# W2 of an encoder's MLP: three of its four groups in seven products with the tokens down the partitions, sums kept in DRAM, and a part of the weight splitting on GpSimd

## The chip, the cores and the metric

The kernel runs on one core of a Trainium2 chip. The metric is the device time of one execution in microseconds. Every time below is read from the runs of the kernel before or from one profiled execution of it.

## The reference

Two layers of an encoder trunk on x of 512 tokens by 1024, all in float32. A layer has an attention half (one input projection, three token mixers, gates and an output projection) and an MLP half. The change lies in the MLP half, in its second matrix, W2 (4096 x 1024):

```python
m = jnp.einsum('bsd,df->bsf', rms_norm(h, mlp_norm[l]), w_mlp_in[l])   # 1024 -> 4096
m = jnp.square(jax.nn.relu(m))
h = h + jnp.einsum('bsf,fd->bsd', m, w_mlp_out[l])                     # 4096 -> 1024
```

## The kernel before

**Numbers.** TensorE multiplies a short form of float32. So each operand is cut in two parts, hi (a cast on ScalarE, ACT) and lo (the operand minus hi, a subtraction on VectorE, DVE), and each product is three matmuls: hi by hi, hi by lo, lo by hi (`passes`, line 568). Weights come by DMA in quarters of 128 x 1024 into two `stage` buffers and are cut into `w_hi` and `w_lo` (`cut_to`, line 512; six buffers of each).

**The MLP half** (`mlp`, line 1335). First come eight units of the output projection (`wo`). Then W1 and W2 run in four groups of 1024 of the 4096 inner columns. W1 goes by pairs of units, four pairs to a group; a pair takes seven products of half size instead of eight (`pair`, line 644; Winograd's form of Strassen's). For that DVE makes sums of the weight blocks (`sa`, `sb` in `cut_pair`, line 535) and adds up the products, which leave PSUM as `c0`, `c1` (shown as `c`); a product has 12 matmuls of 256 columns, a pair 84. The first of those additions, `c<-x,pu`, reads the PSUM tile `x26`, and the pair's last product is written into the same tile.

W2 goes by units: 128 output columns by 512 tokens, eight units to a group, with the weights stationary and the tokens moving. A unit is 24 matmuls of 512 columns (`prod_a`, line 720: 8 blocks of 128 rows, three passes). ACT applies relu and square to each `c` and casts `mh`; DVE makes `ml`. Group 0 copies each unit out of PSUM to a tile `mo` (ACT); groups 1 and 2 add into it (DVE); at the end of group 2 `mo` is scaled and added to h (two more DVE additions a unit); group 3 does the same straight from PSUM and hands h on to the next layer (`ready`) or to the output.

**The order.** The program is first noted down, instruction by instruction. `Plan.order` then lets each engine take the first of its instructions that is ready by a table of costs (`price`), and the outcome is a fixed order for every engine, which the chip runs in order. `mlp_order` (line 52) weaves the first two pairs of the next group's W1 between units of W2 (`WOVEN`). The table does not hold what two engines cost each other when they run side by side.

Of the kernel before, what the change touches and what calls it, by code (L numbers as in the profile page):

```python
# [28 lines left out]
# positions of the small per-layer vectors in the row that every partition receives  # L29
# [20 lines left out]


def mlp_order():
    """W1 goes by pairs of units, W2 by units, in four groups of eight; a group's W1 starts within the W2 before it."""
    pairs = lambda g, k: [("w1", g, 2 * i) for i in k if g < 4]
    seq = pairs(0, range(4))
    for g in range(4):
        n = 0
        for i in range(8):
            while n < len(WOVEN) and WOVEN[n] == i:
                seq += pairs(g + 1, [n])  # L60
                n += 1
            seq.append(("w2", g, i))
# [4 lines left out]
def weight_plan():  # L67
    """Quarters of [128, 1024] in the order in which the core uses them: (key, matrix, rows, columns)."""
# [40 lines left out]
    for what, g, i in mlp_order():  # L109
# [18 lines left out]
AHEAD_LOAD = 6  # L128
AHEAD_SPLIT = 2
# [28 lines left out]
class Ref:  # L158
    """A view of such a tile."""
# [52 lines left out]
def price(engine, op, k):  # L212
    """About how long the engine is held, in ns."""
# [1333 lines left out]
```

## Time and profile before

| | |
|---|---|
| median of 3 runs | 1792.6 us (1791.58 to 1792.85) |
| profiled execution, span of its instructions | 1791.8 us |
| PE (TensorE) busy | 1767.7 us, 99% |
| DVE (VectorE) busy | 1376.4 us, 77% |
| ACT (ScalarE) busy | 983.2 us, 55% |
| POOL (GpSimd) busy | 297.1 us, 17% |

The profile was taken from one execution whose span is 0.8 us below the median of the timed runs. Matmuls are pipelined, so a matmul's own duration overlaps the next one; what a matmul costs is the distance from its start to the next one's. The same holds to a smaller degree for DVE and ACT. In the first layer the MLP half runs from about 518 us (first matmul of `wo`) to 898 us, in the second from 1407 us to the end. The stage just ahead of it, from 404 to 517 us, is the merge of the gates, in which GpSimd adds up gates of 512 columns (`gth`) while DVE cuts the weights of the gates' pairs.

### The profile page before, as it was taken

Reading aid. Unit: us, or ns where it says so; the run is one execution under the profiler, and the core shown is the slowest. Engines: PE = TensorE matmul, PEld = TensorE weight load, DVE = VectorE, ACT = ScalarE, POOL = GpSimd, SP = SyncE. Lnnn points to the kernel's source line nnn. Section 1 sums busy time; section 2 is a strip of 40 time slices with the busy share of each in tenths; the row PEclk is TensorE's granted clock in tenths of the full one; section 3 lists DMA queues with packets and bytes.
Section 4 is the critical chain, followed back from the end, with each engine's and each line's share of the span. In section 5 each row is a group of like instructions: output and inputs, shape, how many; then the busy total and the mean of one; then the engine's idle time right before and its main releaser. Section 6 shows DMA issues by size and latency. Waiting matters only on the chain.

```text
span 1791.8 us, 26264 instructions
## 1 busy us (share of the span) xinstructions
PE 1767.7 (99%) x10216; PEld 1544.8 (86%) x10216; DVE 1376.4 (77%) x2084; ACT 983.2 (55%) x1568; POOL 297.1 (17%) x294
## 2 busy tenths in 40 slices
PE   8999999999999999999999999999999999999999
PEld 6887888889989989999888778888888899989897
DVE  7866797899979766678656677968999797566783
ACT  5545666784446655445444455768844466444450
POOL 3334472002210000000013335700111100000000
PEclk9999999999999999999999999999999999999999
DMA  6311212112352323333432121121133423234331
GB/s 203 105 61 49 93 49 79 59 37 95 107 170 101 118 94 118 123 115 116 152 106 71 48 80 62 59 63 56 39 104 130 159 83 134 95 102 128 121 113 56
DMA packets 53691, 172.50 MB, mean 96 GB/s; under 512 B 6336, under 2 KB 6848, under 8 KB 53568
## 3 DMA queue, kind: packets, MB, share of 16 engines
q1 hardware_dynamic: 53568, 170.84, 29.4%
q8 instruction: 80, 1.31, 0.3%
q14 instruction: 43, 0.35, 0.1%
HBM read 162.43 MB, written 8.39 MB: 95 GB/s over the span
## 4 chain that ended last, share of the span: by engine, by line
PE 82%; DVE 8%; issue 3%; POOL 3%; ACT 2%; DMA 1%; SPq 0%; DVEq 0%; ACTq 0%; POOLq 0%
PE x L411 21%; PE w L411 20%; PE gate L411 6%; PE proj L411 5%; PE wo L411 5%; PE c L411 4%; PE wtr L413 2%; PE rv L411 2%; DVE w_lo L417 2%; PE rg L411 2%; PE rq L411 2%; PE dsc L411 2%; PE gav L411 2%; PE gsc L411 2%; DVE c L417 1%
## 5 line engine op out<-in xcount | busy, mean ns | idle before, releaser
L417 ACT CAST w_hi<-stage 128x1024 fp32r<-128x1024 f32 (+1 forms) x283 | 276.6, 982 | 319.7 <-PE w L411 120.7
L417 DVE TENSOR_TENSOR w_lo<-stage,w_hi 128x1024 fp32r<-128x1024 f32 (+1 forms) x283 | 336.9, 1192 | 78.7 <-ACT w_hi L417 75.8
L411 PE MATMUL x<-u,w_hi 128*128 128x256 f32 x1472 | 273.5, 284 | 5.3 <-DVE c L417 5.3
L411 PEld LDWEIGHTS x<-u,w_hi 128*128 128x128 f32 x1472 | 232.3, 192 | 10.9 <-DVE c L417 8.2
L411 PE MATMUL x<-u,w_lo 128*128 128x256 f32 x736 | 208.0, 283 | 0.0
L411 PE MATMUL w<-ml,w_hi 128*128 128x512 f32 (+1 forms) x520 | 200.3, 386 | 0.0
L411 PE MATMUL w<-mh,w_lo 128*128 128x512 f32 (+1 forms) x520 | 200.1, 386 | 0.0
L411 PE MATMUL w<-mh,w_hi 128*128 128x512 f32 (+1 forms) x520 | 200.1, 387 | 0.0
L411 PEld LDWEIGHTS x<-u,w_lo 128*128 128x128 f32 x736 | 141.1, 192 | 0.0
L417 ACT ACTIVATE c<-c 128x512 f32<-128x512 f32 x156 | 98.4, 631 | 32.9 <-DVE c L417 30.2
L411 PEld LDWEIGHTS w<-mh,w_lo 128*128 128x128 f32 x520 | 97.8, 188 | 19.5
L411 PEld LDWEIGHTS w<-ml,w_hi 128*128 128x128 f32 x520 | 97.8, 188 | 18.7
L411 PEld LDWEIGHTS w<-mh,w_hi 128*128 128x128 f32 x520 | 97.8, 188 | 18.5
L411 PE MATMUL gate<-u,w_hi 128*128 128x512 f32 x320 | 107.3, 399 | 0.0
L411 PE MATMUL x<-t23h,w_lo 128*128 128x256 f32 x368 | 104.2, 283 | 0.0
L411 PE MATMUL x<-t23l,w_hi 128*128 128x256 f32 x368 | 104.0, 283 | 0.0
L411 PE MATMUL x<-t23h,w_hi 128*128 128x256 f32 x368 | 103.9, 283 | 0.0
L417 ACT CAST w_hi<-sa 128x1024 fp32r<-128x1024 f32 x46 | 48.5, 1053 | 77.0 <-DVE sa L417 55.9
L411 PE MATMUL c<-w_hi,u 128*128 128x512 f32 x256 | 86.1, 394 | 0.0
L417 POOL TENSOR_TENSOR gth<-gth,c 128x512 f32<-128x512 f32 x28 | 45.9, 1647 | 179.0 <-DVE c L417 179.0
L417 DVE TENSOR_TENSOR c<-x,pu 128x512 f32<-128x512 f32 x92 | 63.1, 686 | 12.0 <-PE x L411 11.3
L411 PEld LDWEIGHTS x<-t23l,w_hi 128*128 128x128 f32 x368 | 70.6, 192 | 0.0
(278 smaller groups left out, 4554.5 us busy)
## 6 DMA issues: line engine op xcount, KB each, us to landing
stage<-in_w SPq DMA_DIRECT2D x283, 512.0 KB, 3.6
h<-in_x SPq DMA_DIRECT2D x16, 256.0 KB, 5.3
mid<-h SPq DMA_DIRECT2D x16, 256.0 KB, 2.0
h<-mid SPq DMA_DIRECT2D x16, 256.0 KB, 4.8
keep<-h SPq DMA_DIRECT2D x8, 256.0 KB, 4.1
h<-keep SPq DMA_DIRECT2D x8, 256.0 KB, 3.9
out<-h SPq DMA_DIRECT2D x7, 256.0 KB, 2.0
t_ret<-in_t_ret SPq DMA_DIRECT2D x4, 256.0 KB, 4.9
```

The lines of the kernel that those rows point to most:

```text
L411: self.nc.tensor.matmul(k.pop("out"), **k)
L413: self.nc.tensor.transpose(k["out"], k["in_"], k["identity"])
L417: getattr(getattr(self.nc, o.engine), o.name)(**k)
```

## The change

In groups 0, 1 and 2 the eight units of W2 become one product of 1024 by 1024 in seven products of half size (`wide_product`). Now the tokens are stationary, 128 at a time down the partitions, and the weights move, 512 columns at a time. Each of the seven gives 256 tokens by 512 columns, in two PSUM tiles of 128 tokens, with 12 matmuls of 512 columns for each tile, 24 in all. Group 3 stays as it was.

- **Weights** (`cut_wide`): the four blocks A11, A12, A21, A22 of a group's W2 are loaded once, in pieces of 512 columns, and the sums S1 to S4 are made in place on DVE. The hi parts are cast on ACT. The lo parts of the plain blocks A11, A12, A22 (`BESIDE`) are subtracted on GpSimd, 12 pieces to a group; those of the sums on DVE.
- **Tokens** (`rights`): the sums of the token blocks are made in place on DVE, in pieces of 256 columns, and then split into `xh` and `xl`. `mh` and `ml` are gone in these groups.
- **Results**: ACT copies each PSUM tile to `wp`. In group 0 it is stored to DRAM (`sums`) by a DMA of SyncE's queue; in groups 1 and 2 a DMA that GpSimd issues adds it to what lies there. In group 3 `gather` loads the 14 sums back, combines them on DVE (14 additions), turns them with 32 transposes of 128 x 128 on TensorE, and adds to h.
- **Order**: the woven pairs of W1 stand after the second and fourth of the seven products, and the loads are noted where a weight is cut.

```diff
-WOVEN = (3, 6)
+GATHERED = (0, 3)
+WIDE_GROUPS = (0, 1, 2)
+WOVEN = {True: (2, 4), False: (3, 6)}
...
+        elif g not in WIDE_GROUPS:
             a_unit(("w2", g, i), "w_mlp_out", cols(i * 128, 128), r0=g * 1024)
+        elif i == 0:
+            for c in range(2):
+                for j in range(2):
+                    for k in range(2):
+                        r = g * 1024 + j * 512 + k * 256
+                        plan.append((("w2", g, c + 1, j + 1, k), "w_mlp_out", np.arange(r, r + 256), cols(c * 512, 512)))
...
+WIDE = ("A11", "A12", "A22", "S1", "S2", "S4", "S3")
+WIDE_PRODUCTS = (1, 2, 4, 5, 6, 3, 7)
+BESIDE = ("A11", "A12", "A22")
...
+    def cut_wide(self, q, op, k):
+        raw = self.raw
+        def load(x):
+            at = q + (int(x[1]) - 1) * 4 + (int(x[2]) - 1) * 2 + k
+            raw[x, k] = [self.g(x) for _ in range(2)]
+            for i, t in enumerate(raw[x, k]):
+                self.nc.sync.dma_start(out=t, in_=self.a["w"][at][:, i * 512:(i + 1) * 512])
+        def add(x, y):
+            for t, o in zip(raw[x, k], raw[y, k]):
+                self.nc.vector.tensor_tensor(out=t, in0=t, in1=o, op=ALU.add)
+        for x in {"A11": ("A11", "A12"), "A12": ("A22",), "A22": ("A21",)}.get(op, ()):
+            load(x)
+        x = {"S1": "A22", "S2": "A22", "S4": "A12", "S3": "A21"}.get(op, op)
+        if op[0] == "S":
+            add(x, {"S1": "A21", "S2": "A11", "S4": "A22", "S3": "A11"}[op])
+        hi, lo = self.parts(self.p_w, 1024)
+        for i, t in enumerate(raw[x, k]):
+            c = slice(i * 512, i * 512 + 512)
+            self.nc.scalar.copy(out=hi[:, c], in_=t)
+            (self.nc.gpsimd if op in BESIDE else self.nc.vector).tensor_tensor(out=lo[:, c], in0=t, in1=hi[:, c], op=ALU.subtract)
+        return hi, lo
...
-        total = [None] * 8
-        ms = [([], []) for _ in range(4)]
+        ms = [[] for _ in range(4)]
         for what, g, i in mlp_order():
             m = ms[g]
             if what == "w1":
...
                 for c in cs:
                     nc.scalar.activation(out=c, in_=c, func=AF.Relu)
                     nc.scalar.activation(out=c, in_=c, func=AF.Square)
-                    hi, lo = self.g("mh", F32R), self.g("ml", F32R)
-                    self.split(c, hi, lo)
-                    m[0].append(hi)
-                    m[1].append(lo)
+                    if g in WIDE_GROUPS:
+                        m.append(c)
+                        continue
+                    m.append((self.g("mh", F32R), self.g("ml", F32R)))
+                    self.split(c, *m[-1])
                 continue
-            if g == 2:
-                for k in range(3) if i == 0 else range(i + 2, min(i + 3, 8)):
-                    h[k] = load(mid, k)
+            if g in WIDE_GROUPS:
+                if i == 0:
+                    rights = self.rights(m)
+                    nxt = next(rights)
+                now, nxt = nxt, next(rights, None)
+                self.wide_product(l, g, i, now)
+                continue
+            if i == 0:
+                gather = self.gather(h, mid, load, r2)
+            if i in GATHERED:
+                next(gather)
             hi, lo = self.weights(l, ("w2", g, i))
-            if g == 3 and i == 7 and l == L - 1:
-                self.last_unit(hi, lo, m, r2, h[i], ready)
+            m2 = [x[0] for x in m], [x[1] for x in m]
+            if i == 7 and l == L - 1:
+                self.last_unit(hi, lo, m2, r2, h[i], ready)
                 continue
             p = self.psum("mm", "w2")
-            for _ in self.prod_a(p, hi, lo, m, 8, 128):
+            for _ in self.prod_a(p, hi, lo, m2, 8, 128):
                 pass
-            if g == 0:
-                total[i] = self.g("mo")
-                nc.scalar.copy(out=total[i], in_=p)
-            elif g < 3:
-                nc.vector.tensor_tensor(out=total[i], in0=total[i], in1=p, op=ALU.add)
-                if g == 2:
-                    nc.vector.tensor_tensor(out=total[i], in0=total[i], in1=r2, op=ALU.mult)
-                    nc.vector.tensor_tensor(out=h[i], in0=h[i], in1=total[i], op=ALU.add)
+            y = self.g("y")
+            nc.vector.tensor_tensor(out=y, in0=p, in1=r2, op=ALU.mult)
+            nc.vector.tensor_tensor(out=h[i], in0=h[i], in1=y, op=ALU.add)
+            ready(i, h[i])
...
+    def rights(self, m):
+        nc = self.nc
+        lt, rt = slice(0, 256), slice(256, 512)
+        sub = lambda out, x, y: nc.vector.tensor_tensor(out=out, in0=x, in1=y, op=ALU.subtract)
+        t1 = []
+        for n in WIDE_PRODUCTS:
+            if n == 4:
+                for j in range(4):
+                    b1, b2 = m[j], m[4 + j]
+                    if j % 2 == 0:
+                        t1.append(self.g("t1"))
+                    sub(b1[:, rt], b2[:, rt], b1[:, rt])
+                    nc.vector.tensor_tensor(out=b1[:, lt], in0=b1[:, rt], in1=b1[:, lt], op=ALU.add)
+                    sub(b2[:, lt], b2[:, lt], b1[:, lt])
+                    sub(t1[-1][:, j % 2 * 256:j % 2 * 256 + 256], b2[:, rt], b1[:, lt])
+            out = []
+            for i in range(2):
+                hi, lo = self.g("xh", F32R), self.g("xl", F32R)
+                if n == 5:
+                    self.split(t1[i], hi, lo)
+                else:
+                    for j in range(2):
+                        k = 2 * i + j
+                        x = m[k if n in (1, 6, 7) else 4 + k][:, lt if n in (1, 2, 4, 6) else rt]
+                        c = slice(j * 256, j * 256 + 256)
+                        self.split(x, hi[:, c], lo[:, c])
+                out.append((hi, lo))
+            yield out
...
+    def wide_product(self, l, g, o, x):
+        nc, n = self.nc, WIDE_PRODUCTS[o]
+        ps = [self.psum("mm", f"wide{n}") for _ in range(2)]
+        for k in range(2):
+            hi, lo = self.weights(l, ("w2", g, o), k)
+            xh, xl = x[k]
+            for s in range(2):
+                for j in range(2):
+                    t = slice(j * 256 + s * 128, j * 256 + s * 128 + 128)
+                    c = slice(j * 512, j * 512 + 512)
+                    self.passes(ps[s], [(xh[:, t], hi[:, c]), (xh[:, t], lo[:, c]), (xl[:, t], hi[:, c])],
+                                k == 0 and j == 0, k == 1 and j == 1)
+        for s, p in enumerate(ps):
+            y = self.g("wp")
+            nc.scalar.copy(out=y, in_=p)
+            if g == WIDE_GROUPS[0]:
+                nc.sync.dma_start(out=self.sums[n, s], in_=y)
+            else:
+                nc.gpsimd.dma_start(out=self.sums[n, s], in_=y, accum_op=ALU.add)
...
+    def gather(self, h, mid, load, r2):
+        nc = self.nc
+        def back(n, s):
+            x = self.g("wp")
+            nc.sync.dma_start(out=x, in_=self.sums[n, s])
+            return x
+        tt = lambda out, x, y, op=ALU.add: nc.vector.tensor_tensor(out=out, in0=x, in1=y, op=op)
+        u2, c = [None, None], [[None] * 4, [None] * 4]
+        for s in range(2):
+            p1, p2, p6, p5, p3 = (back(n, s) for n in (1, 2, 6, 5, 3))
+            tt(p2, p1, p2)
+            tt(p6, p6, p1, ALU.subtract)
+            tt(p5, p5, p6)
+            tt(p3, p3, p5, ALU.subtract)
+            c[0][s], c[0][2 + s], u2[s] = p2, p3, (p6, p5)
+        for half in range(2):
+            if half:
+                for s in range(2):
+                    p7, p4 = back(7, s), back(4, s)
+                    p6, p5 = u2[s]
+                    tt(p5, p5, p7, ALU.subtract)
+                    tt(p6, p6, p7, ALU.subtract)
+                    tt(p6, p6, p4)
+                    c[1][s], c[1][2 + s] = p6, p5
+            for i in range(4):
+                k = half * 4 + i
+                h[k] = load(mid, k)
+                p = self.psum("tr", "turn")
+                for t in range(4):
+                    self.transpose(p[:, t * 128:(t + 1) * 128], c[half][t][:, i * 128:(i + 1) * 128])
+                y = self.g("y")
+                nc.vector.tensor_tensor(out=y, in0=p, in1=r2, op=ALU.mult)
+                nc.vector.tensor_tensor(out=h[k], in0=h[k], in1=y, op=ALU.add)
+            yield
```

Below, three places in the two kernels' orders. On TensorE, where the first group of W2 in the first layer begins (`x` is a product of W1, `w` one of W2, `wide` one of the seven), before:

```order
L411 MATMUL x_6388<-u_6000,w_lo 128x256
L411 MATMUL w_6498<-mh,w_hi 128x512
L411 MATMUL w_6498<-ml,w_hi 128x512
L411 MATMUL w_6498<-mh,w_lo 128x512
L411 MATMUL w_6498<-mh,w_hi 128x512
L411 MATMUL w_6498<-ml,w_hi 128x512
```

and after:

```order
L457 MATMUL x_6454<-u_6024,w_lo 128x256
L457 MATMUL wide_6562<-w_hi,xh 128x512
L457 MATMUL wide_6562<-w_lo,xh 128x512
L457 MATMUL wide_6562<-w_hi,xl 128x512
L457 MATMUL wide_6562<-w_hi,xh 128x512
L457 MATMUL wide_6562<-w_lo,xh 128x512
```

The unit `w` has become one of the two tiles of the product `wide`; the shape of a matmul, 128 x 512, has stayed.

On GpSimd, from the last gate of the first layer on, before:

```order
L417 TENSOR_TENSOR gth<-gth,c_5507 128x512
L417 TENSOR_TENSOR gth<-gth,c_5568 128x512
L417 TENSOR_SCALAR vmu<-vsum 128x4
L417 TENSOR_TENSOR rs<-ms,mhalf 128x4
L417 TENSOR_SCALAR vmu<-vsum 128x4 x3
```

and after, in the second group, from the fourth piece of A12 on (`A` is a piece of a weight block):

```order
L463 TENSOR_TENSOR w_lo<-A_7110,w_hi 128x512
L463 DMA sums_101<-wp 128x512
L463 DMA sums_102<-wp 128x512
L463 TENSOR_TENSOR w_lo<-A_7216,w_hi 128x512
L463 TENSOR_TENSOR w_lo<-A_7242,w_hi 128x512
L463 TENSOR_TENSOR w_lo<-A_7231,w_hi 128x512
L463 DMA sums_103<-wp 128x512
L463 DMA sums_104<-wp 128x512
L463 TENSOR_TENSOR w_lo<-A_7249,w_hi 128x512
```

Where GpSimd had nothing to do between the gates and the next layer's first unit, it has 36 subtractions and 28 adding DMAs to a layer.

On DVE, ahead of one of the additions `c<-x,pu` in the second group, before:

```order
L417 TENSOR_TENSOR mo<-mo,w_7305 128x512
L417 TENSOR_TENSOR w_lo<-stage,w_hi 128x1024
L417 TENSOR_TENSOR mo<-mo,w_7366 128x512
L417 TENSOR_TENSOR w_lo<-stage,w_hi 128x1024
L417 TENSOR_TENSOR mo<-mo,w_7407 128x512
L417 TENSOR_TENSOR w_lo<-stage,w_hi 128x1024 x2
L417 TENSOR_TENSOR c_7499<-x_7455,pu 128x512
```

and after:

```order
L463 TENSOR_TENSOR A_7242<-A_7242,A_7591 128x512
L463 TENSOR_TENSOR w_lo<-stage,w_hi 128x512
L463 TENSOR_TENSOR A_7231<-A_7231,A_7571 128x512
L463 TENSOR_TENSOR xl<-t_7449,xh 128x512
L463 TENSOR_TENSOR w_lo<-A_7216,w_hi 128x512
L463 TENSOR_TENSOR xl<-t_7593,xh 128x512
L463 TENSOR_TENSOR w_lo<-A_7242,w_hi 128x512
L463 TENSOR_TENSOR c_7736<-x_7681,pu 128x512
```

Here the additions into `mo`, which read PSUM, have given way to sums of weight blocks and to splits, which read two operands from SBUF.

## Rows read from the trace of the kernel before

**Rows 1.** The page: engine, busy us, share of the span, instructions; clock; DMA landing.

```profile
PE 1767.7 (99%) x10216; PEld 1544.8 (86%) x10216; DVE 1376.4 (77%) x2084; ACT 983.2 (55%) x1568; POOL 297.1 (17%) x294
...
PEclk9999999999999999999999999999999999999999
...
h<-in_x SPq DMA_DIRECT2D x16, 256.0 KB, 5.3
```

**Rows 2.** The page: the chain that ended last, by engine.

```profile
PE 82%; DVE 8%; issue 3%; POOL 3%; ACT 2%; DMA 1%; SPq 0%; DVEq 0%; ACTq 0%; POOLq 0%
```

**Rows 3.** Busy us by stretch (PE, PEld, DVE, ACT, POOL), clock, DMA share, GB/s.

```profile
340.00:404.00 64.00, 64.00 (x359) 54.73 (x358) 58.66 (x110) 51.20 (x97) 1.34 (x2) 1.00 0.13 42
...
404.00:517.00 113.00, 110.23 (x764) 102.20 (x763) 106.45 (x139) 51.55 (x71) 24.07 (x14) 1.00 0.39 126
...
666.60:750.60 84.00, 84.00 (x531) 76.39 (x530) 55.33 (x75) 39.48 (x54) 0.00 (x0) 1.00 0.33 106
```

**Rows 4.** The chain in order of time: start us, us, what.

```profile
305.66 0.66 PE wtr L413 x6
...
570.43 30.95 PE x L411 x258
...
604.65 14.53 PE w L411 x64
...
908.04 13.43 PE rv L411 x59
```

**Rows 5.** Timeline of DVE in the second group: start us, us.

```profile
686.10 0.41 DVE L417 TENSOR_TENSOR c<-x,c 128x256 f32<-128x256 f32 x1
686.44 0.68 DVE L417 TENSOR_TENSOR w_lo<-stage,w_hi 128x512 fp32r<-128x512 f32 x1
687.04 1.22 DVE L417 TENSOR_TENSOR w_lo<-sa,w_hi 128x1024 fp32r<-128x1024 f32 x1
688.19 0.69 DVE L417 TENSOR_TENSOR c<-x,pu 128x512 f32<-128x512 f32 x1
```

**Rows 6.** Timeline of DVE in the merge of the gates.

```profile
483.87 0.68 DVE L417 TENSOR_TENSOR sa<-stage 128x512 f32<-128x512 f32 x1
484.47 1.77 DVE L417 TENSOR_TENSOR sb<-stage 128x512 f32<-128x512 f32 x1
486.17 0.68 DVE L417 TENSOR_TENSOR sa<-sa,stage 128x512 f32<-128x512 f32 x1
```

**Rows 7.** Timeline of POOL at the same place.

```profile
484.10 1.60 POOL L417 TENSOR_TENSOR gth<-gth,c 128x512 f32<-128x512 f32 x1 [11.08 <-DVE c L417]
```

**Rows 8.** Groups of DVE, 404 to 517 us: count, busy us, mean ns, idle before.

```profile
L417 DVE TENSOR_TENSOR w_lo<-stage,w_hi 128x1024 fp32r<-128x1024 f32 x17 | 21.8, 1283 | 1.0 <-ACT w_hi L417 0.8
...
L417 DVE TENSOR_TENSOR sb<-stage 128x512 f32<-128x512 f32 x6 | 8.1, 1358 | 0.0
L417 DVE SCALAR_TENSOR_TENSOR mTl<-gth,mTh 128x512 fp32r<-128x512 f32 x6 | 7.4, 1233 | 0.0
...
L417 DVE TENSOR_TENSOR sa<-sa,stage 128x512 f32<-128x512 f32 x6 | 5.2, 861 | 0.0
L417 DVE TENSOR_TENSOR sa<-stage 128x512 f32<-128x512 f32 x5 | 4.8, 967 | 0.2 <-DMA stage<-in_w 0.2
...
L417 DVE TENSOR_TENSOR t23l<-t,t23h 128x512 fp32r<-128x512 f32 x1 | 1.8, 1770 | 0.0
```

**Rows 9.** Waits, 404 to 517 us: us in total, times, longest us.

```profile
PE x L411 <- DVE c L417: 2.8, 4, 0.9
```

**Rows 10.** Groups of DVE and ACT, 666.6 to 750.6 us, columns as in rows 8.

```profile
L417 DVE TENSOR_TENSOR w_lo<-stage,w_hi 128x1024 fp32r<-128x1024 f32 x12 | 14.7, 1225 | 7.5 <-ACT w_hi L417 7.5
...
L417 ACT CAST mh<-c 128x512 fp32r<-128x512 f32 x8 | 5.0, 621 | 0.3
...
L417 DVE TENSOR_TENSOR sb<-stage 128x512 f32<-128x512 f32 x4 | 2.7, 685 | 0.0
...
L417 ACT COPY mo<-w 128x512 f32<-128x512 f32 x1 | 0.6, 577 | 0.0
```

More of the change, by code (lines that the diff above doesn't have):

```diff
@@ L56, in mlp_order @@
     for g in range(4):
-        n = 0
-        for i in range(8):
-            while n < len(WOVEN) and WOVEN[n] == i:
+        n, wide = 0, g in WIDE_GROUPS
+        for i in range(7 if wide else 8):
+            while n < 2 and WOVEN[wide][n] == i:
                 seq += pairs(g + 1, [n])
@@ L122, with steps @@
 PAIRED = {WIDX["w1", f] for f in range(0, 32, 2)} | {WIDX["gate", n, i] for n in GATE_PAIRS for i in range(GATE_PAIRS[n], 8, 2)}
+WIDE = ("A11", "A12", "A22", "S1", "S2", "S4", "S3")
+WIDE_PRODUCTS = (1, 2, 4, 5, 6, 3, 7)
+BESIDE = ("A11", "A12", "A22")
+def steps():
+    out, at = [], {}
+    q = 0
+    while PLAN[q][0][0] != "w1":
+        at[PLAN[q][0]] = len(out)
+        out.append(("pair" if q in PAIRED else "one", q))
+        q += 2 if q in PAIRED else 1
+    for what, g, i in mlp_order():
+        at[(what, g * 8 + i) if what == "w1" else (what, g, i)] = len(out)
+        if what == "w1":
+            out.append(("pair", WIDX["w1", g * 8 + i]))
+        elif g in WIDE_GROUPS:
+            out += [("wide", WIDX["w2", g, 1, 1, 0], WIDE[i], k) for k in range(2)]
+        else:
+            out.append(("one", WIDX["w2", g, i]))
+    return out, at
+STEPS, STEP_AT = steps()
+NS = len(STEPS)
+START = np.cumsum([0] + [2 if s[0] == "pair" else 1 for s in STEPS]).tolist()
+NQS = START[-1]
 BUFS_STAGE = 2
@@ L127 @@
 BUFS_MID = 3
-AHEAD_LOAD = 6
-AHEAD_SPLIT = 2
+AHEAD = 2
 BUFS_G = 51
@@ L242 @@
 class Op:
-    __slots__ = ("engine", "name", "args", "kwargs", "key", "cost", "deps", "tiles", "new", "left", "outs", "end",
-                 "ready")
+    __slots__ = ("engine", "name", "args", "kwargs", "key", "cost", "late", "deps", "tiles", "new", "left", "outs",
+                 "end", "ready")
 class Plan:
@@ L295, in note @@
         o.cost = price(engine, name, kwargs) if engine != "sync" else self.dma_price(kwargs)
+        o.late = self.LATENCY.get(engine, 0.0)
+        if engine == "gpsimd" and name == "dma_start":
+            o.cost, o.late = 960.0, 5000.0
         self.ops.append(o)
@@ L397, in order @@
                 result.append(pick)
-                heapq.heappush(events, (now + o.cost + self.LATENCY.get(e, 0.0), 0, pick))
+                heapq.heappush(events, (now + o.cost + o.late, 0, pick))
                 heapq.heappush(events, (busy[e], 2, pick))
@@ L479, in small, with load @@
         return (self.p_mid if n > 8 else self.p_small).tile(shape, F32, tag=f"s{n}", name=name)
-    def load(self, n):
-        while self.loaded < min(n, L * NQ):
-            q = self.loaded
-            t = self.p_stage.tile([128, 1024], F32, tag="stage", name="stage")
-            self.nc.sync.dma_start(out=t, in_=self.a["w"][q])
-            self.stage[q] = t
-            self.loaded += 1
-    def prefetch(self, i):
-        n = min(i + AHEAD_SPLIT, L * NQ)
-        while self.cut < n:
-            self.load(self.cut + BUFS_STAGE)
-            self.cut_to(self.cut + 1)
-        self.load(min(i + AHEAD_LOAD, self.cut + BUFS_STAGE))
+    def load(self, q, pool=None, tag="stage"):
+        t = (pool or self.p_stage).tile([128, 1024], F32, tag=tag, name=tag)
+        self.nc.sync.dma_start(out=t, in_=self.a["w"][q])
+        return t
+    def prefetch(self, i):
+        end = START[i % NS + 1] + i // NS * NQS + AHEAD
+        while self.cut < L * NS and START[self.cut % NS] + self.cut // NS * NQS < end:
+            i = self.cut
+            kind, q, *more = STEPS[i % NS]
+            q += i // NS * NQ
+            if i not in self.w:
+                self.w[i] = getattr(self, "cut_" + kind)(q, *more)
+            self.cut += 1
     def first_quarter(self, x):
@@ L509, in first_quarter, with parts, cut_one, cut_pair @@
         self.w[0] = parts
[L510 to L527 removed]
+    def parts(self, pool, n):
+        return pool.tile([128, n], F32R, tag="hi", name="w_hi"), pool.tile([128, n], F32R, tag="lo", name="w_lo")
     def part(self, pool, n, t):
[L530 to L531 removed]
+        hi, lo = self.parts(pool, n)
         self.split(t, hi, lo)
         return hi, lo
[L535 removed]
+    def cut_one(self, q):
+        return self.part(self.p_w, 1024, self.load(q))
+    def cut_pair(self, q):
         nc = self.nc
+        q0, q1 = self.load(q), self.load(q + 1)
         lt, rt = slice(0, 512), slice(512, 1024)
@@ L1435, in trunk @@
             tiles.append(k.ref())
+    core.sums = {}
+    for n in WIDE_PRODUCTS:
+        for s in range(2):
+            k = Tile(None, [128, 512], F32, None, "sums")
+            k.real = p_dram.tile([128, 512], F32, name=f"sums{n}{s}")
+            core.sums[n, s] = k.ref()
     def load(src, i):
```

42 lines of the change are left out of this document (8 added, 34 removed).

## The prediction

> **What bounds the kernel now.** I read the page first: TensorE (PE) is busy for 99% of the span at the full clock of 2.4 GHz [rows 1], and of the chain that ended last 82% is PE and 8% VectorE (DVE) [rows 2]. Then the stretches. In a steady group of the MLP (666.6 to 750.6 us) PE is busy for all 84.0 us, DVE for 55.3 (66%), ScalarE (ACT) for 39.5 (47%), GpSimd (POOL) not at all [rows 3]. So PE sets the time there, and fewer matmuls shorten it as long as DVE stays out of the way. How much DVE can be asked for is seen in the merge of the gates just ahead, 404 to 517 us: DVE is busy for 106.45 of 113 us (94%), POOL runs 14 instructions beside it, and PE loses 113 - 110.2 = 2.8 us [rows 3], all of it in four waits for the addition `c` of DVE, the longest 0.9 us [rows 9]. The reader is to see two things: PE forgives a DVE that is nearly full, and it is through `c` that it stops forgiving.
>
> **PE.** Pace is taken from the chain: 64 matmuls of W2 in 14.53 us are 0.227 us each, 258 of W1 (256 columns) in 30.95 us are 0.120, six transposes in 0.66 us are 0.11 [rows 4]. With the weights moving and the tokens stationary the pace is the same: the 59 of `rv` take 13.43 us, 0.228 each [rows 4]. A changed group has 7 x 24 = 168 matmuls of 512 columns in place of 8 x 24 = 192, so 24 x 0.227 = 5.45 us go. Three groups and two layers: 6 x 5.45 = 32.7 us less. The 32 transposes of `gather` cost 32 x 0.11 = 3.5 us a layer, 7.0 in all. PE's own account is 25.7 us shorter, and a steady group has 4 x 84 x 0.120 + 168 x 0.227 = 78.5 us of PE work.
>
> **DVE's account.** Its pace too is the distance of starts: 512 columns 0.60 us (686.44 to 687.04), 1024 columns 1.15 (687.04 to 688.19), 256 columns 0.34 (686.10 to 686.44) [rows 5]. By the new order DVE has in a steady group 62 operations of 512 columns, 12 of 1024 and 52 of 256: 37.2 + 13.8 + 17.7 = 68.7 us. That is 87% of 78.5, after 66%; the splits and sums that the seven products need eat nearly all of the old slack. Without POOL this would still fit, as the merge shows at 94%.
>
> **What GpSimd's subtractions cost DVE.** This is the term that decides. POOL now subtracts 12 pieces of 512 columns a group. In the merge the same kind of work stands beside DVE: when POOL's `gth` starts at 484.10 [rows 7], the DVE operation `sb` that starts at 484.47 takes 1.77 us, while its neighbours `sa`, of the same width, take 0.68 [rows 6]. One such meeting costs DVE 1.09 us. On average it is less. From 404 to 517 us `sb` takes 1358 ns instead of 685, six times; `mTl` 1233 instead of 680, six times; `sa` from itself 861, six times, and from `stage` 967, five times, instead of 684; `w_lo` from `stage` 1283 instead of 1225, 17 times; `t23l` 1770 instead of 684, once [rows 8, 10]. The excess is 4.0 + 3.3 + 1.1 + 1.4 + 1.0 + 1.1 = 11.9 us, over 14 POOL instructions [rows 3] 0.85 us each. I take 0.85; the ends are 0.5 (pieces that fall into idle time of DVE, or beside its additions from PSUM) and 1.09 (every piece in full). The Trainium skill, page "SBUF — State Buffer", section "Who interferes with whom", has a rule that speaks against this change: a DVE instruction with two SBUF inputs contends with a GpSimd instruction that reads SBUF, and whoever comes second blocks until the first is done. The trace agrees with 1.77 against 0.68 us; taken in full, for every piece, it gives the third case below. On DVE itself the 12 pieces would have cost 12 x 0.60 = 7.2 us a group; on POOL they cost it 12 x 0.85 = 10.2.
>
> **Where PE feels it.** By the order almost everything that DVE makes for PE is made over 8 us of PE work ahead; the exception is `c<-x,pu`, which must have read its PSUM tile before PE writes the pair's last product into it, 23 matmuls or 2.76 us later. The addition takes 0.69, so DVE may be 2.0 us late there. I add up DVE's work from one such addition to the next (PE's work in brackets), at 0.85 a piece. First group: 8.5 + 6 x 0.85 = 13.6 (9.6): 4.0 over, 2.0 of it waits; then 19.2 + 5.1 = 24.3 (21.0): 3.3 more wait; then 19.3 (21.2), which recovers. Second and third group, each: 23.1 + 0.85 (26.3) leaves DVE on time; 6.7 + 5 x 0.85 = 10.9 (10.1): 0.8 over; 19.6 + 5.1 = 24.7 (21.0): 4.5 over in all, 2.5 wait; 19.6 (21.0) recovers. A layer waits 5.3 + 2 x 2.5 = 10.3 us, two layers 20.6. At 0.5 a piece the same sums give 1.1 us a layer, at 1.09 18.5.
>
> **The rest, costed near nothing.** ACT in a steady group: 28 casts of weights and 26 of tokens at no more than 0.62 us and 14 copies out of PSUM at 0.58 [rows 10] are 42 us, and about 26 of its present 39.5 [rows 3] stay for W1: at most 68 us of 78.5; from 340 to 404 us ACT was busy for 51.2 of 64 us and PE lost nothing [rows 3]. Price 0; if a copy comes over 2 us late, PE waits for the PSUM tile. POOL's queue: 12 pieces at 1.60 [rows 7] and 14 adding DMAs, whose issue the trace does not show. Between 0 and the 5.3 us that a 256 KB transfer takes to land [rows 1] a DMA, POOL has 19 to 93 us of work a group; I take the 1.60 of its other instructions, 42 us, since an issue moves no data through the engine. Behind a DMA that waits for its `wp` stand pieces of A22 that PE needs some 10 us later. SyncE's queue: 14 stores of `sums` a layer, each waiting for ACT's copy, with loads behind them that are noted two quarters ahead; 0. `gather`: 14 + 16 DVE additions in place of 32 that left groups 1 to 3; 0 to 2 us, taken as 0.
>
> **Sum.** The profiled execution has 1791.8 us: 1791.8 - 25.7 + 20.6 = 1786.7. The median of the runs lies 0.8 higher: 1787 us. So most of what the seven products save, the subtractions on GpSimd take back.
>
> **The rivals.** *Hidden after all.* The pieces meet DVE where it is idle or reads PSUM, at 0.5 each: 2.2 us of waiting, 1791.8 - 25.7 + 2.2 + 0.8 = 1769 us. For it: a quarter of DVE's time is free where the second group's burst begins (6.7 of 10.1). Against it: the six pieces of A12 and A22 then stand where DVE has 19.6 of 21.0. *The full price.* Every piece blocks DVE for 1.09 us: 37 us of waiting, 1791.8 - 25.7 + 37 + 0.8 = 1804 us, slower than before. It turns from gain to loss at about 0.94 a piece, where the waits equal the 25.7. For it: DVE works nearly always from two SBUF operands here, more than in the merge, where a third of its operations read PSUM. Against it: in the merge the 14 cost no more than 11 full meetings would (11.9 / 1.09). *POOL's DMAs.* If an issue held POOL for over 4.2 us, 14 of them and 12 pieces would exceed the 78.5 us of a group, and the pieces of the next would come late; at 5.3 us a group would last 93.4, 14.9 too many, four times: 1767 + 60 = 1827 us. The Trainium skill, "DMA: Bandwidth & Descriptors", section "Latency and other measured facts", puts the first byte of a DMA issued by GpSimd at about 1 us, by which an estimate of POOL's group is 14 + 19 = 33 us and nothing waits; no row here shows it. *No saving at all:* the count of matmuls is certain from the order, and the pace with moving weights is in the rows, so I give this no weight.
>
> **Chances and range.** My forecast, with 0.65 to 1.0 a piece and 1776 to 1797 us, gets 0.58; hidden 0.16; the full price 0.21; POOL's DMAs 0.05. A measurement of this kernel can tell about 0.2% from no change, 1789.0 to 1796.2. Of the forecast 0.36 lies below, 0.20 within, 0.02 above; hidden is all below; the full price 0.01 within and 0.20 above. Faster 0.52, same 0.21, slower 0.27. The range of 1769 to 1804 takes in the bounds of the price of a piece; outside are POOL's DMAs and the tails. The forecast's own range is 1776 to 1797.
>
> **What would show it.** Right: `w_lo` from the pieces of A on POOL at about 1.6 us; DVE's operations of 512 columns beside them at 1.7 to 1.8, and elsewhere 0.68; DVE busy for over 95% of a changed group; PE's idle time in the MLP before `x` on `c`, 2 to 4 us a group, in the halves where POOL subtracts, and next to none in group 3; matmuls of `wide` 0.227 us apart. Wrong: PE waiting for `w_lo` (POOL is late), for `wide` or `turn` on ACT or a DMA (a copy or a sum is late), or a group of 79 us with nothing waiting.

## The result, and the profile after

The changed kernel takes 1837.9 us (median of 4, 1835.2 to 1842.2) against 1792.4: 1.0256 times as long, 95% interval 1.0244 to 1.0269. The forecast was 1787, its range 1769 to 1804. The profiled execution has 1838.6 us, 46.8 more than before; the matmuls alone would have made it 25.7 less, so 72.5 us have to be found.

The page after, the rows that answer to [rows 1, 2], with GpSimd's two new groups (count, busy us, mean ns, idle before):

```profile
PE 1768.0 (96%) x10136; PEld 1542.2 (84%) x10136; DVE 1544.0 (84%) x2428; ACT 1081.1 (59%) x1864; POOL 464.1 (25%) x422
...
PEclk9999999999999899999999999999999999999999
...
PE 64%; DVE 16%; issue 6%; POOL 5%; DMA 4%; ACT 3%; SPq 0%; DVEq 0%; POOLq 0%; ACTq 0%
...
L463 POOL TENSOR_TENSOR w_lo<-A,w_hi 128x512 fp32r<-128x512 f32 x72 | 121.4, 1728 | 297.8 <-ACT w_hi L463 288.6
...
L463 POOL DMA_DIRECT2D sums<-wp x56 | 50.1, 947 | 207.0 <-ACT wp L463 142.9
```

PE's part of the chain fell from 82 to 64%, DVE's doubled, and PEclk has an 8. PE's busy time is as before although 25.7 us of matmuls went: at half clock a matmul of 256 columns takes 0.21 us from start to start (774.20 to 774.41) in place of 0.12. Two rows say it without the tenths, the mean granted clock (before: 1.000) and PE's longest wait by the view of waits (us in total, times, longest):

```profile
core 0: 1838.6 us, clock 0.985
```

```profile
PE x L457 <- DVE c L463: 49.5, 25, 5.2
```

The same row of the kernel before:

```profile
PE x L411 <- DVE c L417: 5.3, 8, 0.9
```

So 49.5 - 5.3 = 44.2 us are new waits; all of PE's idle time (span less busy) grew by 46.5, from 24.1 to 70.6 us. The mean clock puts a bound of (1 - 0.985) x 1838.6 = 27.6 us on what the lower clock took, but a part of that lies in the waits themselves, where it costs nothing more. The sum over the twelve stretches at half clock (us, then PE's busy time):

```profile
sum 54.62, PE 47.77 PEld 44.77 DVE 50.04 ACT 26.74 POOL 5.66; mean PE 3.98 PEld 3.73 DVE 4.17 ACT 2.23 POOL 0.47
```

At half clock 47.8 us of busy PE lose 23.9. With the idle time that is 70.4 of the 72.5.

One whole group of the changed kernel, from the addition `c<-x,pu` in its second group to the one at the same place in its third, beside the untouched merge (columns as in [rows 3]):

```profile
404.00:517.00 113.00, 110.79 (x761) 102.37 (x760) 105.45 (x139) 51.31 (x70) 24.53 (x15) 1.00 0.37 126
...
715.60:807.90 92.30, 82.70 (x504) 75.09 (x504) 79.39 (x127) 56.06 (x102) 30.93 (x26) 0.94 0.56 132
```

The merge is as it was. The group takes 92.3 us where the kernel before took 84.0 [rows 3] and PE has 78.5 us of work. DVE is busy for 79.4 us, which the forecast had (68.7 + 12 x 0.85 = 78.9). But it is idle for 12.9, and in that time nothing is caught up.

The waits of the first layer one by one, on PE's timeline (start us, us, in brackets the idle time before):

```profile
601.02 0.80 PE L457 MATMUL x<-u,w_hi 128*128 128x256 f32 x2 [2.68 <-DVE c L463]
627.11 0.51 PE L457 MATMUL x<-u,w_hi 128*128 128x256 f32 x2 [2.04 <-DVE c L463]
...
691.43 0.38 PE L457 MATMUL x<-t4h,w_hi 128*128 128x256 f32 x1 [2.08 <-DVE c L463]
...
716.37 0.76 PE L457 MATMUL x<-u,w_hi 128*128 128x256 f32 x2 [4.25 <-DVE c L463]
...
773.82 0.58 PE L457 MATMUL x<-t4h,w_hi 128*128 128x256 f32 x1 [5.24 <-DVE c L463]
...
808.63 0.58 PE L457 MATMUL x<-u,w_hi 128*128 128x256 f32 x1 [4.28 <-DVE c L463]
...
862.52 0.39 PE L457 MATMUL x<-t4h,w_hi 128*128 128x256 f32 x1 [1.50 <-DVE c L463]
```

The first two are the first group's, where the sum had 2.0 and 3.3. Those at 716 and 808 stand where it had 2.5. The others, at 691, 773 and 862, it did not have. They are not at `x26`: here the product with `t4h` is to be written into the PSUM tile `x45`, which the pair's addition `c<-x,c` must have read (`z` in `pair`). The one that PE waits for until 691.43:

```profile
690.96 0.41 DVE L463 TENSOR_TENSOR c<-x,c 128x256 f32<-128x256 f32 x1
```

With a fourth of 0.52 us at 679.5 the waits at `x45` make 9.3 of the layer's 22.8 us.

What holds DVE at 701 to 711 us, just ahead of the wait at 716: DVE, then GpSimd.

```profile
701.04 0.69 DVE L463 TENSOR_TENSOR sa<-stage 128x512 f32<-128x512 f32 x1
701.64 3.55 DVE L463 TENSOR_TENSOR c<-c,c 128x256 f32<-128x256 f32 x1
705.12 0.68 DVE L463 TENSOR_TENSOR sb<-stage 128x512 f32<-128x512 f32 x1
...
708.69 2.81 DVE L463 TENSOR_TENSOR sb<-stage,sa 128x512 f32<-128x512 f32 x1
```

```profile
701.73 3.17 POOL L463 TENSOR_TENSOR w_lo<-A,w_hi 128x512 fp32r<-128x512 f32 x2
...
708.99 1.95 POOL L463 TENSOR_TENSOR w_lo<-A,w_hi 128x512 fp32r<-128x512 f32 x1
```

A DVE addition of 256 columns, 0.41 us by itself, takes 3.55 beside two subtractions of GpSimd in a row, and ends after both, although by the rows it began 0.09 us ahead of them.

What follows the wait at 716, by windows (the clock is the third number from the end): the wait, the first 3.4 us behind it, and later.

```profile
711.90:716.35 4.45, 0.21 (x2) 0.01 (x1) 4.45 (x9) 2.18 (x3) 0.00 (x0) 1.00 0.65 159
716.37:719.80 3.43, 3.43 (x14) 3.33 (x15) 3.43 (x6) 1.34 (x2) 0.00 (x0) 0.51 0.08 10
722.70:731.90 9.20, 9.20 (x42) 7.62 (x41) 8.92 (x16) 7.49 (x15) 2.11 (x3) 1.00 0.40 54
```

Here the clock falls to half, to 1.2 GHz, as PE starts again: 14 matmul records in 3.4 us. In the wait at 773 it fell before that:

```profile
768.75:773.75 5.00, 0.00 (x0) 0.00 (x0) 4.87 (x6) 0.00 (x0) 2.60 (x2) 0.73 0.02 3
```

And DVE's own idle time ahead of the wait at 773, on its timeline: first for ACT, then for a load into a stage buffer. ACT's cast, last, had itself waited for a load.

```profile
757.62 1.23 DVE L463 TENSOR_TENSOR w_lo<-stage,w_hi 128x1024 fp32r<-128x1024 f32 x1 [4.39 <-ACT w_hi L463]
...
768.88 1.35 DVE L463 TENSOR_TENSOR sa<-stage 128x512 f32<-128x512 f32 x1 [3.48 <-DMA stage<-in_w]
```

```profile
756.53 1.05 ACT L463 CAST w_hi<-stage 128x1024 fp32r<-128x1024 f32 x1 [2.97 <-DMA stage<-in_w]
```

### The profile page after: what moved, and what is told of

It is laid out like the page before. It is cut to its first block, busy times and chain, and to the rows that moved or that the text cites. A ratio compares the mean times of both kernels' runs of the same rounds, so it can differ in the third digit from the quotient of the medians.

```text
span 1838.6 us, 27271 instructions
## 1 busy us (share of the span) xinstructions
PE 1768.0 (96%) x10136; PEld 1542.2 (84%) x10136; DVE 1544.0 (84%) x2428; ACT 1081.1 (59%) x1864; POOL 464.1 (25%) x422
## 4 chain that ended last, share of the span: by engine, by line
PE 64%; DVE 16%; issue 6%; POOL 5%; DMA 4%; ACT 3%; SPq 0%; DVEq 0%; POOLq 0%; ACTq 0%
PE x L457 12%; PE wide L457 8%; PE gate L457 6%; PE proj L457 5%; PE wo L457 5%; PE w L457 5%; PE c L457 4%; DVE c L463 4%; DMA stage<-in_w 4%; DVE w_lo L463 3%; DVE sb L463 2%; PE wtr L459 2%; PE rg L457 2%; PE gsc L457 2%; PE gav L457 2%
## 5 line engine op out<-in xcount | busy, mean ns | idle before, releaser
L463 ACT CAST w_hi<-stage 128x1024 fp32r<-128x1024 f32 (+1 forms) x235 | 226.3, 967 | 190.4 <-DMA stage<-in_w 100.1
L463 DVE TENSOR_TENSOR w_lo<-stage,w_hi 128x1024 fp32r<-128x1024 f32 (+1 forms) x235 | 280.7, 1197 | 35.7 <-ACT w_hi L463 32.2
L463 POOL TENSOR_TENSOR w_lo<-A,w_hi 128x512 fp32r<-128x512 f32 x72 | 121.4, 1728 | 297.8 <-ACT w_hi L463 288.6
L463 ACT CAST w_hi<-A 128x512 fp32r<-128x512 f32 x168 | 102.0, 620 | 71.7 <-DVE A L463 38.9
L457 PE MATMUL wide<-w_hi,xh 128*128 128x512 f32 x336 | 134.6, 401 | 0.0
L457 PE MATMUL wide<-w_lo,xh 128*128 128x512 f32 x336 | 133.7, 398 | 0.0
L457 PE MATMUL wide<-w_hi,xl 128*128 128x512 f32 x336 | 132.7, 395 | 0.0
L463 POOL DMA_DIRECT2D sums<-wp x56 | 50.1, 947 | 207.0 <-ACT wp L463 142.9
L457 PEld LDWEIGHTS wide<-w_hi,xl 128*128 128x128 f32 x336 | 64.8, 193 | 13.6
L457 PEld LDWEIGHTS wide<-w_hi,xh 128*128 128x128 f32 x336 | 65.6, 195 | 12.6
```

Source lines behind the costliest of these rows:

```text
L457: self.nc.tensor.matmul(k.pop("out"), **k)
L463: getattr(getattr(self.nc, o.engine), o.name)(**k)
```

## The experiments

Three theories stood against each other: GpSimd's subtractions hold DVE, whose lateness PE feels at the tile `x26` (the forecast's own, with the clock added); loads of weights come late; DVE is too full whoever does the subtractions. The edits are shown in short, by what they do.

**Nothing read by GpSimd (e2), nothing added by DMA (e3), neither (e9).** All engines keep their order; only the instruction in its place is another.

```diff
 # e2, e9: in place of GpSimd's 72 subtractions
+nc.gpsimd.memset(w_lo, 0.0)
 # e3, e9: the 56 DMAs store
-nc.gpsimd.dma_start(out=self.sums[n, s], in_=y, accum_op=ALU.add)
+nc.gpsimd.dma_start(out=self.sums[n, s], in_=y)
```

> Every engine's order is kept word for word, but GpSimd's 72 subtractions are replaced by filling the same piece with zeros, which reads nothing (the lo parts of the plain blocks are left out of the result). First theory: VectorE's operations beside them go back to 0.68 us, some 60 us of VectorE's time come back, no wait of TensorE over 1 us is left in the halves with subtractions; the waits for late loads (17 us) and their stretches at half clock (10 us) stay: 1780 to 1800 us. Second theory (late loads alone): over 1825 us.

> Every engine's order is kept, but the 56 adding DMAs of GpSimd store without adding (so the sums of groups 0 and 1 are left out of the result). First theory: 1833 to 1840 us, nothing of note. Second theory, in the form that the adding transfers are what makes the loads of weights land in 7 us in place of 3.5: the waits for loads (17 us) and their half clock (10 us) shrink, 1810 to 1825 us.

> The changed kernel with every engine's order kept, GpSimd's subtractions replaced by filling with zeros and the adding DMAs by plain stores (lo parts of the plain blocks and the sums of groups 0 and 1 are left out of the result). If these two are the whole of what the forecast missed: 1791.8 less 25.7 is 1766, and a few us of late loads: 1766 to 1773 us. If the order itself leaves VectorE late: 1778 us or more.

Measured, in brackets the ratio to the kernel before and its 95% interval: e2 1784.3 us (0.9958, 0.9944 to 0.9973), e3 1822.0 (1.0163, 1.0147 to 1.0178), e9 1769.4 (0.9866, 0.9850 to 0.9883). The same group as above, from the same addition to the same, in e2, e3 and e9:

```profile
695.90:776.70 80.80, 78.78 (x506) 71.91 (x505) 69.96 (x128) 55.66 (x102) 18.16 (x26) 1.00 0.63 153
```

```profile
713.50:800.60 87.10, 82.24 (x504) 74.80 (x504) 79.10 (x127) 56.02 (x102) 27.39 (x26) 0.96 0.40 140
```

```profile
694.80:773.65 78.85, 78.77 (x506) 71.88 (x506) 70.05 (x127) 55.75 (x102) 13.60 (x26) 1.00 0.47 155
```

With both taken away a group lasts 78.85 us, PE's own 78.5, and the program comes to 1769.4, 2.5 us above what the matmuls alone promise (1792.6 - 25.7 = 1766.9). The hold costs 1837.9 - 1784.3 = 53.6 us, the adding 16.0; both together 68.5. The fills are shorter than the subtractions too (GpSimd is busy for 18.2 us of e2's group, 30.9 of the changed kernel's), but e1 below, where GpSimd has neither, gains as much. DVE's busy time in the group falls from 79.4 to 70.0 us without the reads, so a piece cost it 9.4 / 12 = 0.79. The Trainium skill, "SBUF — State Buffer", section "Who interferes with whom", says that such a DVE instruction contends with a GpSimd instruction that reads SBUF and not with one that only writes; the fills of e2 agree. By my expectation e3 should have moved nothing under the first theory; so the second theory holds a share. In e3's trace the place of the wait at 773 shows it: DVE's two waits ahead of it are 1.30 and 0.85 us in place of 4.39 and 3.48, and PE waits 2.06 in place of 5.24:

```profile
768.41 0.39 PE L458 MATMUL x<-t4h,w_hi 128*128 128x256 f32 x1 [2.06 <-DVE c L464]
```

**All subtractions on DVE (e1), and without adding (e7, e1's order kept).**

```diff
-BESIDE = ("A11", "A12", "A22")
+BESIDE = ()
```

> The 12 subtractions a group that the change gave to GpSimd are put back on VectorE; the order is planned anew. First theory (GpSimd's subtractions hold VectorE, which comes late to the addition that frees the tile x26; TensorE waits, and its clock falls to half behind the wait): a piece costs VectorE 0.60 us in place of 0.87, the waits in the halves with subtractions fall from 29.5 us in two layers to under 8, and seven of twelve stretches at half clock go (about 14 us): 1790 to 1805 us. Second theory (late loads of weights into the two stage buffers): 1825 to 1840 us, since the loads stay as they are. Third (VectorE is simply too full, whoever holds it): 7.2 us more of its own work a group, 1835 us or more.

> The kernel with all subtractions on VectorE (its order kept word for word), but the 56 adding DMAs store without adding (the sums of groups 0 and 1 are left out of the result). With the subtractions on GpSimd the same edit gave 16 us. If it did so because the adding transfers delay the loads of weights: 5 to 10 us again, 1775 to 1781 us. If because the shorter issues shift GpSimd's subtractions, or the half clock: nothing here, 1783 to 1788 us.

e1: 1785.7 us (1778.8 to 1793.7 in ten runs; 0.9965, 0.9952 to 0.9978), 52 less than with GpSimd, below the 1790 to 1805 of the first theory, and the fastest that still computes everything (f2 and e8 below are level with it). The third theory falls: DVE has 7.2 us more of its own work in a group, and the time goes down. e7: 1774.5 (0.9901, 0.9886 to 0.9916), another 11.2 less, a little more than the 5 to 10 expected of late loads. PE's waits in the first layer's MLP in e1, and what the adding takes of the DMA engines there (GpSimd's queue: packets, MB, share of 16 engines), in e1 and then in e7:

```profile
PE x L457 <- DVE w_lo L463: 3.4, 3, 1.5
PE wide L457 <- ACT wp L463: 0.9, 1, 0.9
```

```profile
q0 software_dynamic: 4032, 7.34, 14.1%
```

```profile
q0 software_dynamic: 2240, 7.34, 5.6%
```

For the same 7.34 MB the adding DMAs occupy the engines two and a half times as long. DVE's waits for loads into the stage buffers in that stretch are 5.7 us in e1 and 0.4 in e7; PE's wait for `w_lo` goes with them. The traced run of e1 took 1778.8 us, 6.9 below its median, and lies 5.3 above that of e7; so these rows account for about half of the 11.2 us, and where the rest lies was not seen.

**The tile x26 (f1), and with the subtractions on DVE (f2).** PSUM has a bank that lies idle in the MLP; the pair's last product is written there.

```diff
+        y = self.psum("av", "x3")
         self.product(y[:, lt], w, u, 3)
```

> The changed kernel, but the last product of a pair of W1 goes to a PSUM tile of its own in the bank that lies idle in the MLP, so that it no longer waits for the addition c<-x,pu; the order is planned anew, GpSimd keeps its subtractions. If the tile x26 is where TensorE feels a late VectorE: most of the 49 us of waits and 26 us at half clock go, and what is left is VectorE's own load, about 79 us in a group of 78.5: 1780 to 1800 us. If VectorE's total is the bound wherever the wait shows: 1815 to 1835 us.

> Both: the last product in a bank of its own, and the 12 subtractions a group on VectorE. VectorE has 75.9 us of work in a group of 78.5, and TensorE no tight place left before the weights: nearly all of the 25.7 us saved by the matmuls shows, 1767 to 1775 us. If the loads of weights are a cause of their own: 1775 to 1785 us.

f1: 1842.4 us (1.0276, 1.0261 to 1.0292); f2: 1786.4 (0.9969, 0.9958 to 0.9981), as e1. Both are above both of their ranges, and nothing is gained. In f1 the wait at the same place (716 us above) stands at the next product that needs a late addition, the one into `x45`:

```profile
720.24 0.58 PE L457 MATMUL x<-t4h,w_hi 128*128 128x256 f32 x1 [4.80 <-DVE c L463]
```

All of f1's waits for `c` in the first layer's MLP are at `x45`. So `x26` is where a late DVE is noticed first, and not why it costs. My theory fell in this part.

**What a wait costs (e5, e6).** The kernel before, its order kept; DVE makes the addition `c<-x,pu` of each of W1's 32 pairs five or nine times over.

```diff
 # when the addition is issued
+for _ in range(4):      # e6: 8
+    add(two(c0), two(y), wide(tmp[:, lt]))
```

> The kernel before, every engine's order kept, but VectorE makes each addition c<-x,pu of W1's 32 pairs five times over (the same sum into the same tile), which holds the tile x26 some 2.4 us longer. By my reading of the slack (2.0 us) TensorE waits 0.4 to 1 us at each of 32 pairs, 13 to 32 us in all. First theory with the clock: no wait is long enough to bring the clock down, so the time rises by the waits alone: 1805 to 1825 us. If any wait at all halves the clock: over 1850 us.

> As the run before, but nine times over: the tile is held 4.8 us longer, and TensorE waits about 2.8 us at each of 32 pairs, 90 us. First theory with the clock (behind such a wait TensorE runs some 3.5 us at half clock, which costs 1.6 us): 32 x 4.4 = 140 us, 1915 to 1940 us. If a wait costs only itself: 1875 to 1890 us.

e5: 1856.5 us (1.0353, 1.0338 to 1.0368); e6: 1994.2 (1.1125, 1.1109 to 1.1142). PE's waits for `c`, of e5 and of e6:

```profile
PE x L412 <- DVE c L419: 51.0, 48, 2.2
```

```profile
PE x L412 <- DVE c L419: 139.4, 40, 4.7
```

In e5 the span grew by 62.2 us, of which 45.7 are these waits (51.0 - 5.3), at a mean clock of 0.996, which is at most (1 - 0.996) x 1854.0 = 7.4 us more; the last 9 us are only in part explained (the view counts a wait from the modelled end of a matmul, and is 0.16 us short of the one shown below). In e6 it grew by 198.8, of which the waits are 134.1: the other 65 us, 2.0 to a wait, come behind them, where the clock is at half. One of e6's waits (the clock falls in it), what follows and what comes then, by windows:

```profile
724.30:728.89 4.59, 0.34 (x3) 0.14 (x2) 4.39 (x8) 0.00 (x0) 0.00 (x0) 0.81 0.00 0
728.95:734.20 5.25, 5.19 (x19) 4.66 (x20) 5.25 (x11) 2.42 (x3) 0.00 (x0) 0.52 0.15 19
734.20:736.00 1.80, 1.80 (x15) 1.76 (x14) 0.70 (x2) 1.36 (x3) 0.00 (x0) 1.00 0.85 348
```

Behind this wait of 1.45 us in e5 the clock stays whole:

```profile
685.20:686.65 1.45, 0.08 (x1) 0.00 (x0) 1.38 (x4) 0.00 (x0) 0.00 (x0) 1.00 0.48 186
686.65:690.00 3.35, 3.25 (x27) 3.26 (x28) 2.92 (x6) 1.60 (x3) 0.00 (x0) 1.00 0.23 51
```

Between them no line can be drawn from these runs: after the wait of 2.08 us at 691 in the changed kernel the clock fell (0.63 from 691.43 to 695.85), after the same wait in e3 it did not (1.00). By its time e5 is in the second range, over 1850, but not for that range's reason: not every wait halved the clock. e5 and e6 came out above what I had expected because the waits were longer than I had sized them. From the last matmul's start to the next, the wait shown of e5 is 1.75 us and that of e6 4.65; less the pace of 0.12, 1.6 and 4.5. So, by these two waits, four additions more hold the tile for 2.9 us, not 2.4, and DVE may be 2.9 - 1.6 = 1.3 us late there, not 2.0.

**Where the loads are held up (e4, e8, f4, f5, f13, f14).** A third stage buffer beside GpSimd's subtractions (e4) and without them (e8):

```diff
-BUFS_STAGE = 2
-BUFS_G = 51
+BUFS_STAGE = 3
+BUFS_G = 49
```

> A third stage buffer of 128 x 1024 for loaded weights, with two fewer of the 51 general tiles; the order is planned anew. First theory with the loads as a second, smaller cause: the waits of TensorE that follow a late load (about 9 us a layer) and their half clock go, those in the halves with subtractions stay: 1808 to 1822 us. First theory alone: 1833 to 1840. Second theory: under 1800 us.

> All subtractions on VectorE and a third stage buffer (two general tiles fewer; planned anew). If the waits that are left (9 us of waiting and 5 us at half clock in the profiled execution) are those of loads that start only when one of two stage buffers comes free: 1771 to 1779 us. If the loads wait behind other loads in SyncE's queue, or the order is what matters: 1783 us or more.

e4: 1850.3 us (1.0327, 1.0301 to 1.0354), slower than the change itself; e8: 1785.6 (0.9966, 0.9956 to 0.9975), as e1. My account of e4 fell: a third buffer gains no time. In e8's trace PE's waits for `w_lo`, over the whole program, are 0.3 us in place of e1's 4.9, but those of `wide` for ACT's copy are 4.4 in place of 2.7; the time stays where it was. e4 is planned anew and has two general tiles fewer; which of these its 12 us are is open.

Loads of W2's pieces and of the sums issued by GpSimd (f4), or those of the sums alone (f5), with all subtractions on DVE:

```diff
-nc.sync.dma_start(out=x, in_=self.sums[n, s])
+nc.gpsimd.dma_start(out=x, in_=self.sums[n, s])
```

> All subtractions on VectorE; the pieces of W2 and the sums that gather loads back are issued by GpSimd in place of SyncE, so that the loads into the stage buffers stand behind none of them. If the queue of SyncE makes the loads late: 1768 to 1778 us. If the transfers themselves take the time: 1783 us or more.

> As the run before, with the sums that gather loads back alone moved to GpSimd. The waits of the last group (3 to 4 us a layer with their half clock) should go, those at the other groups' starts stay: 1777 to 1783 us; if the queue is not the cause, 1785 us or more.

f4: 1801.0 us (1.0050, 1.0032 to 1.0068); f5: 1790.0 (0.9989, 0.9980 to 0.9999): both slower than e1. DVE's waits for loads into the stage buffers in the first layer's MLP, 5.7 us in e1, are 10.9 in f4, though those loads now stand behind no loads of W2's pieces or of the sums in SyncE's queue. So standing behind them is not what makes loads late; what GpSimd's issues cost in its place is not separated.

Two PSUM tiles of a product stored or added by one DMA with rows of 4 KB (f13; f14 with one tile of results instead of two):

```diff
-y = self.g("wp")                                          # 128 x 512, twice
+y = self.p_wp.tile([128, 1024], F32, tag="wp2", name="wp2")
```

> All subtractions on VectorE; the two PSUM tiles of a product are copied into one tile of 128 x 1024 (two such tiles, four general tiles fewer; planned anew) and stored or added by one DMA with rows of 4 KB, 28 adding DMAs in place of 56, the same bytes. If the adding transfers cost by row: their share of the DMA engines falls from 14% towards 7% in the MLP, and about half of the 11 us that plain stores gave comes: 1778 to 1782 us. If by bytes: the share stays, 1785 us or more.

> The same with a single tile of 128 x 1024 for the results and two general tiles fewer. If the tile is free again before the next product is copied: as the run before. If TensorE or ScalarE must wait for the transfer to have read it: some us more, 1783 to 1792 us.

f13: 1791.3 us (0.9991, 0.9982 to 1.0001); f14: 1794.0 (1.0005, 0.9995 to 1.0014). The same row of GpSimd's queue, in f13:

```profile
q0 software_dynamic: 2016, 7.34, 12.1%
```

Half the packets, and still 12.1 of 14.1%: the adding takes its share by the bytes more than by the row. What makes f13 5.5 us slower than e1 stays open; its order was planned anew, with four general tiles fewer.

**The hold where DVE has room (e10).** The kernel before, order kept, 72 extra subtractions on GpSimd from a stage buffer into a spare tile.

```diff
+self.nc.gpsimd.tensor_tensor(out=spare, in0=stage[:, r], in1=w_hi[:, r], op=ALU.subtract)
```

> The kernel before, every order kept, with 36 extra subtractions of 512 columns a layer on GpSimd, 12 to each of groups 0 to 2 of W2, from a loaded weight and its hi part into a spare tile. If the hold decides only where VectorE is nearly full: VectorE gets 60 us busier in the trace (0.6 to 1.1 a piece), and since it has 29 us of slack a group the time stays, 1791 to 1797 us. If the hold by itself makes the addition that frees x26 late: 1805 us or more.

1813.2 us (1.0113, 1.0097 to 1.0128), 20.7 more. But it doesn't tell the two apart. DVE's busy time grew by only 1402.2 - 1376.4 = 25.8 us, 0.36 a piece: DVE is idle for a third of such a group and many of its operations there read PSUM, and the run doesn't divide the two. And GpSimd's reading held the stage buffers longer. DVE's waits for loads in the first layer's MLP, in e10 and in the kernel before:

```profile
DVE sa L418 <- DMA stage<-in_w: 16.1, 10, 4.7
```

```profile
DVE sa L417 <- DMA stage<-in_w: 4.2, 2, 3.7
```

The time rose although DVE is busy for only 66% of such a group [rows 3]; by which of the two stays open.

**Two groups of four in seven products (f12).** All subtractions on DVE, half the adding DMAs.

```diff
-WIDE_GROUPS = (0, 1, 2)
+WIDE_GROUPS = (0, 1)
```

> Two groups of four in seven products in place of three, all subtractions on VectorE, half the adding DMAs; the sums are gathered in the third group. The matmuls save 4 x 5.45 less 7.0 us of transposes, 14.8; with 3 to 6 us lost to late loads: 1781 to 1784 us. If the third group's load on VectorE was what cost the rest of the gain: 1776 to 1779 us.

1794.6 us (1.0011, 1.0000 to 1.0021): the 14.8 us are lost again, in 11.4 - 5.3 = 6.1 us of added waits for `c`, 4.7 for `w_lo` and 3.5 for `wide`, with some half clock behind them (the traced run, at 1799.4 us, lies 4.8 above the median). That is above both expected ranges; the cause stays open.

## Why the prediction was wrong, point by point

**PE.** Right. 25.7 us: e9's group lasts 78.85 us where 78.5 was worked out, its program 1769.4 where PE's account gives 1766.9.

**DVE's account and the price of a piece.** Right. 68.7 us a group without GpSimd, measured 70.0; 0.85 a piece, measured 0.79. The value taken was the nearest of the three, and the full price of 1.09 is not it. So the miss does not come from the price of a piece but from what a late DVE costs: the hold cost 53.6 us where 20.6 of waits were forecast, 33.0 too few, and the adding 16.0 where nothing was, together 49.0 of the 51 missed.

**Where PE feels it.** This is the step that failed, in four ways.

First, it added up DVE's work between two points as if DVE never stood still itself. At 78.9 us of work for PE's 78.5 no slack is left in the group, and then each wait of DVE for ACT's cast, for a load or for PE counts: 12.9 us in the group shown, of which the two rows at 757 and 768 us are 7.9, both behind late loads. PE's waits for `c` in the first layer's MLP are 22.8 us, where the sum had 10.3.

Second, it gave a wait no price beyond its length. Behind the longer ones PE ran at 1.2 GHz, and this took 23.9 us, more than the 20.6 us that were forecast as waits. It also feeds back: with PE at half clock behind the wait at 691 the casts into weight tiles that `wide` still read came later, and DVE stood 1.44 us at 697.9, just ahead of the 4.25 us at 716. In e3, where the clock held at that place, DVE did not stand there, and the wait that follows is 2.80 us. ACT's cast and DVE's subtraction, in the changed kernel and then in e3:

```profile
696.85 1.05 ACT L463 CAST w_hi<-sb 128x1024 fp32r<-128x1024 f32 x1 [3.05 <-PE wide L457]
697.93 1.23 DVE L463 TENSOR_TENSOR w_lo<-sb,w_hi 128x1024 fp32r<-128x1024 f32 x1 [1.44 <-ACT w_hi L463]
```

```profile
695.63 1.05 ACT L464 CAST w_hi<-sb 128x1024 fp32r<-128x1024 f32 x1 [1.47 <-PE wide L458]
696.76 1.22 DVE L464 TENSOR_TENSOR w_lo<-sb,w_hi 128x1024 fp32r<-128x1024 f32 x1
```

Third, it put the room for a late `c<-x,pu` at 2.0 us; e5 and e6 have it at about 1.3.

Fourth, it took `c<-x,pu` and its tile for the only tight place. `c<-x,c` and `x45` are a second one, with 9.3 of the 22.8 us. With `x26` out of the way (f1) the time did not fall, since the next product waits for the same late DVE.

**The rest, costed near nothing.** Wrong in one row. GpSimd's issue of an adding DMA takes 0.95 us (I took 1.60 within 0 to 5.3), and that rival is out. But the transfers cost 16.0 us beside the subtractions, 11.2 without them. Of their work on the DMA engines I had counted nothing, and gave no reason, only how long the issue held GpSimd.

**The rivals.** *The full price* had the right side, at 1804, by a price that did not come: the loss was to begin at 0.94 a piece (0.92 by the forecast's own sums), and it came at 0.79. *Hidden after all* gives its 1769 only once the hold and the adding are both gone (e9).

## What to carry to other kernels

Where an off-path engine is asked for as much as the pacing engine has, don't sum its work between two points: sum its work and its own waits, and don't count on a group without slack: here 78.9 us of DVE's work for PE's 78.5 made 92.3. The waits of TensorE in e6, 4.2 us on the mean, cost their length and 2 us more, for the half clock behind them. A subtraction moved to GpSimd, which reads SBUF beside VectorE's own reads, cost VectorE 0.79 us in place of the 0.60 that it takes there; here it relieved VectorE of nothing.

## What was not expected of the hardware

A DVE addition of 256 columns that met two subtractions of GpSimd in a row took 3.55 us: it ended after both. GpSimd's fills of the same pieces cost DVE next to nothing (70.0 us in the group, of 68.7 worked out). An adding DMA into DRAM took two and a half times the share of the DMA engines that a plain store of the same bytes took (14.1 against 5.6%), and half as many, longer rows brought it only to 12.1%. Its effect was seen far from it, in VectorE and TensorE waiting behind loads of weights that came late.
